# Attention heads by pairs: the half-array products of two heads given together, alternating between the halves of the TensorE array

## The chip, the cores and the metric

The kernel runs on one core of a Trainium2 chip, in one launch. The metric is the device time of that core in microseconds (us), the median of the runs of a kernel.

## What is computed

Two layers' worth of a hybrid language model on 256 tokens of width 1024, in float32 (a sketch of the reference, cut to the parts that matter here):

```python
# first block
u_ssm, q, k, v = split(rmsnorm(x) @ w_in)
y_ssm  = s5_branch(u_ssm)          # recurrence over 256 tokens, 32 groups of 64 complex states, gelu, glu
y_attn = stick_breaking(q, k, v)   # 8 heads of 64:
#   z = q k^T / 8;  A = sigmoid(z) * prod_{s<j<t} (1 - sigmoid(z_j));  out = A v, s < t only
merged = g_ssm * (y_ssm @ w_up_ssm) + g_attn * (y_attn @ w_up_attn)    # g: sigmoid gates of u
h = x + merged @ w_out
h = h + relu(rmsnorm(h) @ w_ff1) ** 2 @ w_ff2
# second block, twice: gated feed-forward, a mixer, gated feed-forward
# the mixer: softmax attention (8 heads, 96 query and key features, 64 value features) beside a second
# attention with compressed and plain keys; gates; projections; layer norms
```

## The kernel before, in words

**Products.** Weights come from memory as float32 blocks. ScalarE copies half a block to its rounded high part (`high`, L538), VectorE subtracts to get the low part (`low`, L553), and a large product is three TensorE products of high and low parts (`mm3`, L590 to L592); "a trio" below. The small products of the attentions are plain float32, and the trace shows each of these as two passes.

**Heads on half the array.** A head of 64 features fills half of the 128 x 128 array. In `stick` (stick-breaking attention), the scores of head h (`sz`, L1268 and L1269) contract over 64 rows, the upper or the lower half by the head's parity; its output (`so`, L1308 and L1310) has 64 columns, left or right. In `mla_head` (the mixers' softmax attention) the output (`mo`, L1887 and L1888) has 64 columns as well. The rest of a head lies between them: in `stick` three ScalarE functions and three VectorE operations (tiles `sa`, `szs`), a cumulative sum as a product (`sc`, L1288 to L1290), two VectorE operations, an exponential.

**The order.** The engines run what stands in their queues in order. For the first block and each mixer, a planner (`Flow`) writes these orders when the program is built: streams (generators) state the engine, an estimated time and the buffers that the next piece needs; the piece that could start first by the planner's estimate is given out, the lower priority number winning among those that are close. Where TensorE would wait, it gives out trios of "fillers", in a fixed list: in the first block the input products, the eight gate products (`g0` to `g7`), then the glu (`lu`, L590 on tile `sg`), the attention's projection (`a0`, `a1`, on `oa`) and the recurrence's (`s0`, `s1`). The glu needs the gelu of the recurrence's outputs (`s5_gelu`: after all heads and all four groups), the attention's projection needs `joined` (all pairs and the gelu), the last two need the glu.

**Buffers.** Streams must hold tiles of the planner's lists: `t2` (4 at the start of the first block, 2 more come free in `s5_powers`, which keeps one), `acc` (5 PSUM tiles), `sunit` (1: one head of the stick-breaking attention at a time), `grp` (2 groups of the recurrence at a time). A head holds two `t2`, `sa` until `sc`, `szs` until `so`. A group of the recurrence (`s5_states`) takes one `t2` with its inputs' product (`s5b`, L1161), turns them on VectorE (L1152) and GpSimd (L1169, L1170), then needs two more `t2` at once for a factor (`s5r`, L1175) and the scans (L1179); it turns the result (L1152, GpSimd L1189 and L1190) and adds its outputs to PSUM (`ys`, L1205 and L1208). Heads have priorities 3 to 10, groups 8 to 11.

Of the kernel before, what the change touches and what calls it, by code (L numbers as in the profile page):

```python
# [17 lines left out]
P = 128  # L18
# [7 lines left out]
# The tail of a layer: its last TAIL row blocks, row by row; the products after which the first row's two  # L26
# halves are transposed, in feed-forward layers and in the others.
# [3 lines left out]
# Of Flow: buffers, priorities, and what it weighs (times in us).  # L31
# [10 lines left out]
# The first block's later products: gates, glu and the two projections.  # L42
LATE = "g0 g1 g2 g3 g4 g5 g6 g7 lu a0 a1 s0 s1".split()
# The weight stream: blocks loaded in halves, tiles split ahead, split blocks at a mixer's end.
# [3 lines left out]
# When a feed-forward layer's first hidden columns are turned (without and with gate), and when the  # L48
# weights of a mixer's first products are taken.
# [4 lines left out]
def host_constants():  # L54
    """Tables that depend on the shapes alone."""
# [39 lines left out]
class Halves:  # L95
    """Columns of a row in two tiles."""
# [10 lines left out]
class Row:  # L107
    """The end of a layer for 128 tokens: their sums on top of the residual, the norm
    (of the root mean square, or of mean and variance when there is a bias) and the
    feature-major split of the result."""  # L110
# [31 lines left out]
    def finish(self):  # L142
        """Up to the scale of the rows; then self.piece(c0, c1) writes the result."""
        k, nc, s, b = self.k, self.k.nc, self.s, self.b
        TS, STT = nc.vector.tensor_scalar, nc.vector.scalar_tensor_tensor
        m = self.n - 1
        if self.bB is None:
            TS(s(10), s(4), s(4 + m), self.eps, OP.add, OP.add)
            k.rsqrt(s(11), s(10))
            return  # L150
        TS(s(12), s(0), s(m), 1.0 / D, OP.add, OP.mult)
        TS(s(13), s(9), s(12), None, OP.add)
        TS(s(13), s(13), s(13), -self.eps, OP.mult, OP.add)
        TS(s(10), s(4), s(4 + m), s(13), OP.add, OP.subtract)  # L154
        k.rsqrt(s(11), s(10))
        for c in (slice(0, 512), slice(512, D)):
            STT(self.h[:, b, c], self.h[:, b, c], s(12), self.gB[:, c], OP.subtract, OP.mult)
# [12 lines left out]
    def turn(self, c0, c1, pool=None):  # L170
        """Transposes columns c0:c1 and splits the high parts; returns the low parts' step."""
# [12 lines left out]
    def early(self):  # L184
        """All of it but the transposes."""
# [8 lines left out]
    def late(self, head):  # L194
        """All of it, the next layer's work on the other tokens filling the wait."""
# [15 lines left out]
class FFHead:  # L211
    """The first 256 hidden columns of a feed-forward layer, token by token."""
# [40 lines left out]
class MixHead:  # L253
    """The first columns of a mixer's input product, token by token."""
# [21 lines left out]
def act(n, exp=False):  # L276
    """A ScalarE instruction's time, in us, for n columns."""
# [3 lines left out]
def dve(n, fast=False):  # L281
    """A VectorE instruction's time, in us, for n columns."""
# [3 lines left out]
class Flow:  # L286
    """An order of emission for streams of work that share the engines. A stream is a generator that
    yields (engine, time, resources...) before it emits that work, or the name of a signal to wait for;
    the next piece is the one that could start first by a model of the engines, and fillers (feature-major
    products) go where TensorE would wait. Each resource is a count of buffers with the times at which  # L290
    they come free."""
# [24 lines left out]
    def rest(self):  # L316
        """Puts off the current stream, whose products are too small to keep TensorE's clock up."""
# [6 lines left out]
    def start(self, s):  # L324
        """When a stream's next piece could start, or None."""
# [26 lines left out]
    def weight(self, e):  # L352
        """The next part of the weights' split, as a stream's piece."""
# [26 lines left out]
    def filler(self, t):  # L380
        """A step of the first filler."""
# [13 lines left out]
    def evac(self, engine, d, f):  # L395
        """Work that follows the filler's products."""
        self.evacs.append((self.free["PE"] + 0.65, engine, d, f))

    def open(self):
        """Whether a filler can go on."""  # L400
# [51 lines left out]
class Kern:  # L452
    def __init__(self, ctx, tc, A, out):
# [8 lines left out]
        self.blocks = []      # planned weight blocks, in the order of their use  # L462
        self.staged = []      # loaded, not yet split
        self.loaded = 0
        self.pieces = 0       # halves of blocks split so far
# [36 lines left out]
    def rowblk(self, w, r0, nk, c0, n):  # L502
        """nk chunks of 128 rows from r0, n columns from c0, as [128, nk, n]."""
# [26 lines left out]
    def high(self):  # L530
        """The high part of half a weight block."""
# [9 lines left out]
    def piece(self):  # L541
        """The low part of half a weight block, and the high part of the next."""
# [43 lines left out]
    def mm3(self, out, l, r, start, stop, **kw):  # L586
        """out (+)= l.T @ r, the operands split in high and low parts."""
# [6 lines left out]
    def split_from(self, hi, lo, src, scale=None):  # L594
        """hi, lo (float32r) from src (* scale)."""
# [8 lines left out]
    def fm_gen(self, key, xs, evac, alloc=None):  # L604
        """A feature-major block: [128, 256] sums per 128 columns, in PSUM tiles of
        two; evac(i, tile) follows each tile. Yields the tiles of work done."""
# [27 lines left out]
    def fill(self, tiles):  # L634
        """Emits about that much of the waiting work."""
# [9 lines left out]
    def tok_mm(self, o, w, xs, k0, b, c0, c1, first, last, **kw):  # L645
        """Adds a row block to the token-major sums o of the 128 tokens b, columns c0:c1."""
# [9 lines left out]
    def tok_first(self, o, ws, b, n):  # L656
        """The token-major sums o of n columns, the tokens' low parts last."""
# [15 lines left out]
    def tok_tail(self, accs, parts, rows, head, at):  # L673
        """The last row blocks (w, xs, k0): the first 128 tokens, then the others,
        each followed by the end of its row."""
# [24 lines left out]
    def bcast_row(self, src, n, name):  # L700
        """A row of DRAM on every partition."""
# [13 lines left out]
    def transpose_split(self, src, nchunk, xs):  # L715
        """src: [128 tok, 2, nchunk*128] -> split feature-major xs."""
# [155 lines left out]
    # The states' recurrence runs over 64 steps of four tokens each: state' = a^4 state + V [u], and  # L872
    # the outputs of a step are W state + K [u], with V, W and K made of B, C and the powers of a.
    # Its inputs and outputs sit on the partitions as (token of the step, channel of 32).
# [26 lines left out]
    def s5_powers(self, f):  # L901
        """The powers of a and what goes with them: s5c (parameters by state), pw, dk, tau4, r4."""
# [70 lines left out]
        def cmul(out, x, y, n):  # L973
            """out = x * y, complex; x: n numbers per state chunk, y: one."""
# [13 lines left out]
    def s5_part(self, f, dst, x, y, k, s0, s1):  # L988
        """dst (block-diagonal) = y_k * x; s0, s1: the signs' operations."""
# [13 lines left out]
    def s5_b(self, f):  # L1003
        """The states' inputs: bb (for K) and its transpose."""
# [20 lines left out]
    def s5_c(self, f):  # L1025
        """The outputs' weights by state, and their transpose for K."""
# [36 lines left out]
    def s5_turns(self, f):  # L1063
        """The steps' rotations."""
# [21 lines left out]
    def s5_k(self, f):  # L1086
        """K: row blocks by the token that enters, column blocks by the one that leaves."""
# [45 lines left out]
    def s5_in(self, ps, u4, q0):  # L1133
        """The products' columns (two blocks of 128 channels) as the steps' inputs."""
# [8 lines left out]
    def s5_states(self, f, g, u4, ys):  # L1143
        """Four chunks of 128 states (groups 8g to 8g + 7) over all steps, and their part of the outputs
        in the PSUM accumulators ys, two [128, 8, 64]."""
# [3 lines left out]
        def turn(m, v):  # L1149
            """m: the real and the imaginary parts v by cos and by sin."""  # L1150
# [62 lines left out]
    def s5_gelu(self, f, ys, out):  # L1213
        """gelu of the outputs, by channel and token, and its split."""
# [5 lines left out]
        # the steps' inputs, rotations and K are done with  # L1220
# [32 lines left out]
    def stick(self, f, h, qk, vt, O):  # L1253
        """One head of the stick-breaking attention; a pair's result takes its queries' place in qk."""
        nc = self.nc
        pair, hh = divmod(h, 2)
        rows = slice(64 * hh, 64 * hh + 64)
        q, k = qk[rows, pair, :], qk[rows, 4 + pair, :]
# [7 lines left out]
        yield "PE", 0.65, "acc", "t2", "t2", "sunit"  # L1266
        z = self.acc("sz")
        nc.tensor.matmul(z[:, :T], k[:, :P], q, start=True, stop=True)  # L1268
        nc.tensor.matmul(z[:, T:T + P], k[:, P:], q[:, P:], start=True, stop=True)  # L1269
        f.sig("sz%d" % h)  # L1270
# [4 lines left out]
        yield "ACT", 3 * act(384) + 0.4  # L1275
# [21 lines left out]
        nc.scalar.activation(zs, zs, AF.Exp)  # L1297
        f.sig("st%d" % h)
        yield "vt"
        if hh:  # L1300
            yield "so%d" % pair
            yield "PE", 0.65
        else:
            yield "PE", 0.65, "acc"
            O[pair] = self.acc("so")
        o = O[pair]
        hv = slice(h * 64, (h + 1) * 64)
        nc.tensor.matmul(o[rows, :T], vt[:, 0, hv], zs[:, :T], start=True, stop=False,  # L1308
                         tile_position=(0, 64 * hh))
        nc.tensor.matmul(o[rows, P:T], vt[:, 1, hv], zs[:, T:], start=False, stop=True,  # L1310
# [941 lines left out]
```

## Time and profile before

| | |
|---|---|
| median of 3 runs | 1560.99 us (1559.63 to 1564.06) |
| profiled execution, first to last instruction | 1560.2 us; the profile gives no other time of that execution |
| TensorE busy, products | 1534.7 us, 98% of the span |
| VectorE / ScalarE / GpSimd busy | 992.3 / 773.2 / 97.8 us (64 / 50 / 6%) |
| DMA | 265.24 MB, mean 170 GB/s |
| mean granted TensorE clock | 0.994 |

The stick-breaking heads and the recurrence run between about 48 and 168 us of the span, the glu and the projections from 177 to 205 us, the two mixers' heads around 660 to 695 and 1235 to 1263 us.

### The profile page before, as it was taken

How to read it: one execution, taken by the hardware profiler on the slowest of the kernel's cores; microseconds unless marked ns; L12 is line 12 of the kernel's file. 1: busy time of each engine (PE TensorE's matmuls, PEld its weight loads, DVE VectorE, ACT ScalarE, POOL GpSimd, SP SyncE). 2: the span in 40 equal slices, each digit the busy share in tenths (PEclk: the TensorE clock that was granted, in tenths of full speed). 3: DMA queues.
4: the chain of work that ended last, by engine and by line, in shares of the span. 5: the costliest groups of instructions: out<-in, count | busy, mean ns of one | idle time of the engine just before them, and what ended most of it. 6: DMA issues, size and time to landing. Idle time of an engine off the chain costs nothing.

```text
span 1560.2 us, 25562 instructions
## 1 busy us (share of the span) xinstructions
PE 1534.7 (98%) x10637; PEld 1418.5 (91%) x10637; DVE 992.3 (64%) x1572; ACT 773.2 (50%) x1259; POOL 97.8 (6%) x112
## 2 busy tenths in 40 slices
PE   8799999999999999999999999999999999999998
PEld 7699989989999998989999999999999999899997
DVE  7956776454654547778875445844557779864544
ACT  7455845444543435557654343534434567554342
POOL 2841000000000000000000000000000000000000
PEclk9899999999999999999999999999999999999999
DMA  7413355556564555532565655565546433565550
GB/s 215 154 62 122 136 197 186 197 172 207 179 225 163 186 183 176 192 103 88 188 216 189 204 175 189 191 210 170 185 152 216 136 108 125 181 225 189 188 190 28
DMA packets 188597, 265.24 MB, mean 170 GB/s; under 512 B 10441, under 2 KB 154817, under 8 KB 188482
## 3 DMA queue, kind: packets, MB, share of 16 engines
q1 hardware_dynamic: 186466, 256.27, 49.7%
q0 software_dynamic: 2016, 7.34, 1.4%
q8 instruction: 84, 1.38, 0.4%
q14 instruction: 31, 0.25, 0.0%
HBM read 262.55 MB, written 1.05 MB: 169 GB/s over the span
## 4 chain that ended last, share of the span: by engine, by line
PE 92%; DVE 4%; POOL 2%; ACT 1%; issue 1%; DMA 0%; DVEq 0%; SPq 0%; ACTq 0%
PE mm L590 16%; PE mm L591 16%; PE mm L592 16%; PE acc L591 8%; PE acc L592 8%; PE acc L590 8%; PE head L664 6%; DVE wsplit L553 1%; PE tp L177 1%; PE cps L1665 1%; PE in L590 1%; PE in L592 1%; PE in L591 1%; PE apt L1949 1%; PE mo L1887 1%
## 5 line engine op out<-in xcount | busy, mean ns | idle before, releaser
L553 DVE TENSOR_TENSOR wsplit<-st,wsplit 128x1024 fp32r<-128x1024 f32 (+1 forms) x482 | 562.0, 1210 | 184.4 <-ACT wsplit L538 184.0
L590 PE MATMUL mm<-xh,wsplit 128*128 128x256 f32 x2000 | 572.2, 286 | 0.0
L591 PE MATMUL mm<-xl,wsplit 128*128 128x256 f32 x2000 | 564.8, 282 | 0.0
L592 PE MATMUL mm<-xh,wsplit 128*128 128x256 f32 x2000 | 564.8, 282 | 0.0
L538 ACT ACTIVATE wsplit<-st 128x1024 fp32r<-128x1024 f32 (+1 forms) x482 | 471.7, 1036 | 30.6 <-DMA st<-in_ffn_wg_dram 11.9
L590 PEld LDWEIGHTS mm<-xh,wsplit 128*128 128x128 f32 x2000 | 378.9, 189 | 4.5 <-issue 1.1
L591 PEld LDWEIGHTS mm<-xl,wsplit 128*128 128x128 f32 x2000 | 379.0, 189 | 2.1
L592 PEld LDWEIGHTS mm<-xh,wsplit 128*128 128x128 f32 x2000 | 378.6, 189 | 0.2 <-DVE wsplit L553 0.2
L590 PE MATMUL acc<-wsplit,ffh 128*128 128x512 f32 x480 | 189.5, 395 | 0.0
L592 PE MATMUL acc<-wsplit,ffl 128*128 128x512 f32 x480 | 189.4, 395 | 0.0
L591 PE MATMUL acc<-wsplit,ffh 128*128 128x512 f32 x480 | 189.3, 394 | 0.0
L828 ACT ACTIVATE fff<-mm 128x512 f32<-128x512 f32 x55 | 32.9, 598 | 280.1 <-PE mm L592 280.1
L832 DVE TENSOR_TENSOR fff<-fff,mm 128x512 f32<-128x512 f32 x55 | 37.9, 688 | 174.4 <-PE mm L592 111.2
L598 ACT ACTIVATE ffh<-fff 128x512 fp32r<-128x512 f32 x55 | 34.8, 632 | 165.8 <-DVE fff L832 165.8
L592 PEld LDWEIGHTS acc<-wsplit,ffl 128*128 128x128 f32 x480 | 90.4, 188 | 21.0
L590 PEld LDWEIGHTS acc<-wsplit,ffh 128*128 128x128 f32 x480 | 90.4, 188 | 18.8
L591 PEld LDWEIGHTS acc<-wsplit,ffh 128*128 128x128 f32 x480 | 90.4, 188 | 18.7
L707 POOL TENSOR_TENSOR rowst<-rowst,neghalf 128x1 f32<-128x1 f32 x18 | 14.7, 817 | 1227.2 <-DVE rowst L154 946.8
L664 PE MATMUL head<-wsplit,xh 128*128 128x256 f32 (+2 forms) x416 | 66.1, 311 | 0.0
L664 PEld LDWEIGHTS head<-wsplit,xh 128*128 128x128 f32 x416 | 59.6, 188 | 3.5
L599 DVE TENSOR_TENSOR ffl<-fff,ffh 128x512 fp32r<-128x512 f32 x55 | 38.1, 693 | 38.4 <-ACT ffh L598 38.4
L181 ACT ACTIVATE xh<-tp 128x256 fp32r<-128x256 f32 (+1 forms) x46 | 18.6, 470 | 48.6 <-PE tp L177 48.6
(405 smaller groups left out, 1894.6 us busy)
## 6 DMA issues: line engine op xcount, KB each, us to landing
st<-in_ffn_wg_dram SPq DMA_DIRECT2D x44, 1024.0 KB, 5.6
st<-in_ffn_wu_dram SPq DMA_DIRECT2D x44, 1024.0 KB, 5.4
st<-in_ffn_wd_dram SPq DMA_DIRECT2D x44, 1024.0 KB, 5.0
st<-in_w_ff_dram SPq DMA_DIRECT2D x32, 1024.0 KB, 6.4
st<-in_w_in_dram SPq DMA_DIRECT2D x23, 1024.0 KB, 6.3
st<-in_w_out_dram SPq DMA_DIRECT2D x12, 1024.0 KB, 4.9
st<-in_w_gate_dram SPq DMA_DIRECT2D x8, 1024.0 KB, 5.5
st<-in_w_in_dram SPq DMA_DIRECT2D x10, 512.0 KB, 5.4
```

The lines of the kernel that those rows point to most:

```text
L177: nc.tensor.transpose(ps[:, c * P:(c + 1) * P], self.out[:, b, c0 + c * P:c0 + (c + 1) * P], k.ident)
L181: nc.scalar.activation(hi, v, AF.Copy)
L538: self.nc.scalar.activation(self.split[i][0][:, a, b], self.staged[i][:, a, b], AF.Copy)
L553: self.nc.vector.tensor_tensor(lo[:, a, b], st[:, a, b], hi[:, a, b].bitcast(F32), OP.subtract)
L590: nc.tensor.matmul(out, lh, rh, start=start, stop=False, **kw)
L591: nc.tensor.matmul(out, lh, rl, start=False, stop=False, **kw)
L592: nc.tensor.matmul(out, ll, rh, start=False, stop=stop, **kw)
L598: nc.scalar.activation(hi, src, AF.Copy)
L599: nc.vector.tensor_tensor(lo, src, hi.bitcast(F32), OP.subtract)
L664: self.nc.tensor.matmul(o, l, r, start=i == 0, stop=i == len(ops) - 1)
L828: nc.scalar.activation(f, ps, AF.Silu if gated else AF.Relu)
L832: nc.vector.tensor_tensor(f, f, ps, OP.mult)
```

## The change

In `stick`, the even head of a pair now asks for the scores' tiles of both heads (two `acc`) and gives out the four `sz` products, alternating between the halves of the array; the odd head takes its two `t2` when its first ScalarE function comes. The even head ends after its exponential; the odd head waits for both and gives out the four `so` products, alternating, after which both heads' `szs` and the one `sunit` are given back. So `sunit` now stands for a pair. In `mla_head` likewise: the odd head gives out the four `mo` products. The number and the shapes of products stay.

```diff
     def stick(self, f, h, qk, vt, O):
...
-        yield "PE", 0.65, "acc", "t2", "t2", "sunit"
-        z = self.acc("sz")
-        nc.tensor.matmul(z[:, :T], k[:, :P], q, start=True, stop=True)
-        nc.tensor.matmul(z[:, T:T + P], k[:, P:], q[:, P:], start=True, stop=True)
-        f.sig("sz%d" % h)
+        if hh == 0:
+            yield "PE", 0.9, "acc", "acc", "t2", "t2", "sunit"
+            for i in range(2):
+                O[h + i] = self.acc("sz")
+            for c in range(2):
+                for i, r in enumerate(half):
+                    q, k = qk[r, pair, :], qk[r, 4 + pair, :]
+                    nc.tensor.matmul(O[h + i][:, c * T:T + c * P], k[:, c * P:c * P + P], q[:, c * P:],
+                                     start=True, stop=True)
+            f.sig("sz%d" % h)
+        else:
+            yield "sz%d" % (h - 1)
+        z = O[h]
...
-        yield "ACT", 3 * act(384) + 0.4
+        yield ("ACT", 3 * act(384) + 0.4) + (("t2", "t2") if hh else ())
...
+        O[h] = zs
         f.sig("st%d" % h)
+        if hh == 0:
+            return
         yield "vt"
-        if hh:
-            yield "so%d" % pair
-            yield "PE", 0.65
-        else:
-            yield "PE", 0.65, "acc"
-            O[pair] = self.acc("so")
...
+        yield "st%d" % (h - 1)
+        yield "PE", 0.9, "acc"
+        o = self.acc("so")
+        for c in range(2):
+            for i, r in enumerate(half):
+                hv = slice((h - 1 + i) * 64, (h + i) * 64)
+                nc.tensor.matmul(o[r, c * P:T], vt[:, c, hv], O[h - 1 + i][:, c * T:T + c * P],
+                                 start=c == 0, stop=c == 1, tile_position=(0, 64 * i))
+        f.put("t2", "t2", "sunit")
...
     def mla_head(self, f, h, qkT, vm, out, om):
...
+        out[h] = pt
         if hh == 0:
-            yield "PE", 0.65, "acc"
-            out[pair] = self.acc("mo")
+            f.put("unit")
+            f.sig("pt%d" % h)
         else:
-            yield "mo%d" % pair
-            yield "PE", 0.65
-        o, r0 = out[pair], 64 * hh
...
+            yield "pt%d" % (h - 1)
+            yield "PE", 0.9, "acc"
+            o = self.acc("mo")
+            for c in range(2):
+                for i in range(2):
+                    r0 = 64 * i
+                    nc.tensor.matmul(o[r0:r0 + 64, c * P:T], vm[:, c, h - 1 + i],
+                                     out[h - 1 + i][:, c * T:T + c * P], start=c == 0, stop=c == 1,
+                                     tile_position=(0, r0), skip_group_check=True)
+            f.put("t2", "t2", "unit")
```

The planner moves much of the first block with it. Three places matter below. The first is the end of the heads. VectorE before, from the last head's last operation to the gelu's split (`s5y` are the copies of the gelu, L1243):

```order
L1294 SCALAR_TENSOR_TENSOR szs<-const_82,szs 128x2x128
L553 TENSOR_TENSOR wsplit<-st,wsplit 128x1024
L1243 COPY s5y<-s5g 32x256 x8
L1250 TENSOR_TENSOR sg<-s5y,sg 128x512
L553 TENSOR_TENSOR wsplit<-st,wsplit 128x1024
```

And with the change, directly after the last head's last operation:

```order
L1179 SCALAR_TENSOR_TENSOR s5s<-s5r,s5z 128x256 x2
L1152 TENSOR_TENSOR s5m<-s5s,csT 128x512 x2
L1179 SCALAR_TENSOR_TENSOR s5s<-s5r,s5z 128x256 x2
L1152 TENSOR_TENSOR s5m<-s5s,csT 128x512 x2
L553 TENSOR_TENSOR wsplit<-st,wsplit 128x1024 x2
L1152 TENSOR_TENSOR s5m<-s5b,csT 128x512 x4
L553 TENSOR_TENSOR wsplit<-st,wsplit 128x1024
L1179 SCALAR_TENSOR_TENSOR s5s<-s5r,s5z 128x256 x2
L1152 TENSOR_TENSOR s5m<-s5s,csT 128x512 x2
L1179 SCALAR_TENSOR_TENSOR s5s<-s5r,s5z 128x256 x2
L1152 TENSOR_TENSOR s5m<-s5s,csT 128x512 x2
L1243 COPY s5y<-s5g 32x256 x8
```

All four groups of the recurrence, which VectorE had done among the heads before, now have their scans behind the last head, and two of them their inputs too. On TensorE the same groups stand behind the last `so`: 14 trios, half of the first group's `ys`, 2 trios, and then, in a row:

```order
L1205 MATMUL ys<-u_184,s5kT 128x64
L1208 MATMUL ys<-s5x,s5wT 128x63 x2
L1205 MATMUL ys<-u_184,s5kT 128x64
L1208 MATMUL ys<-s5x,s5wT 128x63 x2
L1161 MATMUL s5b<-u_184,s5bT 128x64 x8
L1205 MATMUL ys<-u_184,s5kT 128x64
L1208 MATMUL ys<-s5x,s5wT 128x63 x2
L1205 MATMUL ys<-u_184,s5kT 128x64
L1208 MATMUL ys<-s5x,s5wT 128x63 x2
L1161 MATMUL s5b<-u_184,s5bT 128x64 x8
L590 MATMUL mm<-xh,wsplit 128x256
```

After that last row's 4 trios come the `ys` of the two late groups and at once the glu; the 4 trios are the last of the gate products. Before, all `ys` stood among the heads, and 26 trios stood between the last `so` and the glu.

The second place is ScalarE from the gelu's split to the tanh of the glu (`gl`) and the high part of the attention's result (`oah`). Before:

```order
L1248 ACTIVATE sg<-s5y 128x512
L538 ACTIVATE wsplit<-st 128x1024 x2
L1531 ACTIVATE oah<-H 128x1024
L1431 ACTIVATE gates<-mm,s5c 128x256 x2
L1465 ACTIVATE gates<-gates 128x4096
L538 ACTIVATE wsplit<-st 128x1024 x2
L1471 ACTIVATE gl<-gl 128x1024
```

With the change:

```order
L1248 ACTIVATE sg<-s5y 128x512 x2
L538 ACTIVATE wsplit<-st 128x1024
L1470 ACTIVATE gates<-gates 128x4096
L1476 ACTIVATE gl<-gl 128x1024
L1536 ACTIVATE oah<-H 128x1024
```

The attention's result is now split after the tanh of the glu instead of before it. VectorE follows: its part `oal` stood before the copies `gl`, and now stands behind them, two weight splits and one operation of the glu (`s5y`):

```order
L1451 TENSOR_SCALAR gl<-mm,s5c 128x256 x4
L553 TENSOR_TENSOR wsplit<-st,wsplit 128x1024 x2
L1478 SCALAR_TENSOR_TENSOR s5y<-gl,s5y 128x1024
L1538 TENSOR_TENSOR oal<-H,oah 128x1024
```

The third place is VectorE at the end of the recurrence's projection (`mt`: the merge of one tile of it), just before the output product `w_out`. Before:

```order
L602 SCALAR_TENSOR_TENSOR xl<-mt_1972,xh 128x512
L553 TENSOR_TENSOR wsplit<-st,wsplit 128x1024 x2
L1497 SCALAR_TENSOR_TENSOR mt_2018<-gates,mm 128x512
L1499 TENSOR_TENSOR mt_2018<-mt_2018,gates 128x512
L602 SCALAR_TENSOR_TENSOR xl<-mt_2018,xh 128x512
L1497 SCALAR_TENSOR_TENSOR mt_2023<-gates,mm 128x512
L1499 TENSOR_TENSOR mt_2023<-mt_2023,gates 128x512
L602 SCALAR_TENSOR_TENSOR xl<-mt_2023,xh 128x512
L553 TENSOR_TENSOR wsplit<-st,wsplit 128x1024 x7
```

With the change:

```order
L602 SCALAR_TENSOR_TENSOR xl<-mt_2012,xh 128x512
L1502 SCALAR_TENSOR_TENSOR mt_2017<-gates,mm 128x512
L1504 TENSOR_TENSOR mt_2017<-mt_2017,gates 128x512
L602 SCALAR_TENSOR_TENSOR xl<-mt_2017,xh 128x512
L553 TENSOR_TENSOR wsplit<-st,wsplit 128x1024 x10
```

By the last merge VectorE has made 45 weight halves before and 42 with the change; the 43rd and 44th are the first block of `w_out`.

## Rows read from the trace of the kernel before

**Rows 1.** The page: busy time of the engines, and the chain that ended last.

```profile
PE 1534.7 (98%) x10637; PEld 1418.5 (91%) x10637; DVE 992.3 (64%) x1572; ACT 773.2 (50%) x1259; POOL 97.8 (6%) x112
...
PE 92%; DVE 4%; POOL 2%; ACT 1%; issue 1%; DMA 0%; DVEq 0%; SPq 0%; ACTq 0%
```

**Rows 2.** TensorE's waits, whole span, the one at the glu: us, times, longest.

```profile
PE mm L591 <- DVE sg L1250: 0.7, 1, 0.7
```

**Rows 3.** Timeline of TensorE, 97 to 99.4: start, us, engine, line, operation.

```profile
97.20 0.28 PE L592 MATMUL mm<-xh,wsplit 128*128 128x256 f32 x1
97.41 0.65 PE L1308 MATMUL so<-szs,vt 128*64 128x256 f32 x2
...
98.21 0.70 PE L1268 MATMUL sz<-H 64*128 64x256 f32 x2
...
99.05 0.39 PE L590 MATMUL mm<-xh,wsplit 128*128 128x256 f32 x1
99.28 0.27 PE L591 MATMUL mm<-xl,wsplit 128*128 128x256 f32 x1
```

**Rows 4.** Timeline of TensorE, 1235.3 to 1237.2: two heads' outputs, one after the other in program.

```profile
1235.79 0.70 PE L1887 MATMUL mo<-apT,vm 128*64 128x256 f32 x3
...
1236.32 0.38 PE L1887 MATMUL mo<-apT,vm 128*64 128x256 f32 x1
...
1236.85 0.55 PE L1873 MATMUL apt<-const,ap 128*128 128x128 f32 x3
```

**Rows 5.** Timelines of VectorE and GpSimd, 117 to 124: one group of the recurrence.

```profile
117.50 1.26 DVE L1179 TENSOR_TENSOR_SCAN s5s<-s5r,s5z 128x256 f32<-128x256 f32 x2
118.69 1.26 DVE L1152 TENSOR_TENSOR s5m<-s5s,csT 128x512 f32<-128x512 f32 x2
...
120.12 0.74 POOL L1189 TENSOR_TENSOR s5x<-s5m 128x256 f32<-128x256 f32 x1 [5.98 <-DVE s5m L1152]
...
121.50 0.73 POOL L1169 TENSOR_TENSOR s5z<-s5m 128x256 f32<-128x256 f32 x1
...
122.87 0.62 POOL L1175 TENSOR_TENSOR s5r<-constt,s5q 128x256 f32<-128x256 f32 x1
```

**Rows 6.** Timeline of TensorE, 106 to 108.4: half of a group's `ys`, then the next product.

```profile
106.19 0.33 PE L1205 MATMUL ys<-u,s5kT 128*128 128x64 f32 x2
...
107.57 0.65 PE L1308 MATMUL so<-szs,vt 128*64 128x256 f32 x2
```

**Rows 7.** Timeline of ScalarE, 165 to 178: gelu, copies, split; then the attention's result.

```profile
166.43 1.09 ACT L1228 ACTIVATE s5g<-ys 128x512 f32<-128x512 f32 x2
...
167.66 5.43 ACT L1241 ACTIVATE s5y<-s5g 32x256 f32<-32x256 f32 x8
173.12 0.63 ACT L1248 ACTIVATE sg<-s5y 128x512 fp32r<-128x512 f32 x1
...
177.74 1.05 ACT L1531 ACTIVATE oah<-H 128x1024 fp32r<-128x1024 f32 x1
```

**Rows 8.** Timeline of VectorE, 166 to 184: two weight splits, the glu's copies.

```profile
177.21 2.36 DVE L553 TENSOR_TENSOR wsplit<-st,wsplit 128x1024 fp32r<-128x1024 f32 x2
...
182.55 0.88 DVE L1446 TENSOR_SCALAR gl<-mm,s5c 128x256 f32<-128x256 f32 x2 [1.07 <-PE mm L592]
```

**Rows 9.** Timeline of VectorE, 196 to 207: the merge of one tile.

```profile
196.80 0.69 DVE L1497 SCALAR_TENSOR_TENSOR mt<-gates,mm 128x512 f32<-128x512 f32 x1 [0.97 <-PE mm L592]
...
198.92 0.69 DVE L602 SCALAR_TENSOR_TENSOR xl<-mt,xh 128x512 fp32r<-128x512 f32 x1 [0.70 <-ACT xh L601]
```

**Rows 10.** Busy time by stretch: length; engines PE, PEld, DVE, ACT, POOL; granted clock.

```profile
48.90:51.25 2.35, 0.00 (x0) 0.00 (x1) 2.35 (x4) 2.33 (x4) 2.29 (x3) 0.97 0.37 89
51.25:57.90 6.65, 6.65 (x28) 6.24 (x28) 6.65 (x8) 4.68 (x6) 6.52 (x6) 0.50 0.36 126
...
73.10:78.40 5.30, 5.26 (x19) 4.57 (x20) 5.30 (x5) 2.49 (x3) 5.18 (x4) 0.50 0.61 185
```

**Rows 11.** The same view of TensorE alone, the fillers behind the last `so`.

```profile
166.30:175.70 9.40, 9.40 (x80) 1.00 0.31 113
```

More of the change, by code (lines that the diff above doesn't have):

```diff
@@ L1256, in stick @@
         pair, hh = divmod(h, 2)
-        rows = slice(64 * hh, 64 * hh + 64)
-        q, k = qk[rows, pair, :], qk[rows, 4 + pair, :]
+        half = (slice(0, 64), slice(64, P))
         def diag(a):
@@ L1297, in stick @@
         nc.scalar.activation(zs, zs, AF.Exp)
+        O[h] = zs
         f.sig("st%d" % h)
+        if hh == 0:
+            return
         yield "vt"
-        if hh:
-            yield "so%d" % pair
-            yield "PE", 0.65
-        else:
-            yield "PE", 0.65, "acc"
-            O[pair] = self.acc("so")
[L1306 to L1310, printed above, removed]
-                         tile_position=(0, 64 * hh))
-        f.put("t2", "sunit")
-        f.sig("so%d" % pair)
-        if hh:
-            yield "sz%d" % (h - 1)
-            yield "ACT", act(256)
-            nc.scalar.activation(qk[:, pair], o[:, :T], AF.Copy)
-            f.put("acc")
-            f.sig("sp%d" % pair)
+        yield "st%d" % (h - 1)
[7 more added lines that the diff above has]
+        f.put("t2", "t2", "sunit")
+        yield "ACT", act(256)
+        nc.scalar.activation(qk[:, pair], o[:, :T], AF.Copy)
+        f.put("acc")
+        f.sig("sp%d" % pair)
     def first_block(self):
@@ L1878, in mla_head @@
         f.put("acc")
+        out[h] = pt
         if hh == 0:
-            yield "PE", 0.65, "acc"
-            out[pair] = self.acc("mo")
-        else:
-            yield "mo%d" % pair
-            yield "PE", 0.65
-        o, r0 = out[pair], 64 * hh
-        kw = dict(tile_position=(0, r0), skip_group_check=True)
-        nc.tensor.matmul(o[r0:r0 + 64, :T], vm[:, 0, h], pt[:, :T], start=True, stop=False, **kw)
-        nc.tensor.matmul(o[r0:r0 + 64, P:T], vm[:, 1, h], pt[:, T:], start=False, stop=True, **kw)
-        f.sig("mo%d" % pair)
-        f.put("t2", "unit")
-        if hh == 1:
+            f.put("unit")
+            f.sig("pt%d" % h)
+        else:
+            yield "pt%d" % (h - 1)
[8 more added lines that the diff above has]
+            f.put("t2", "t2", "unit")
             if not om:
```

## Prediction

> **What bounds the kernel now.** The page first: TensorE is busy for 98% of the span and makes 92% of the chain that ended last [rows 1]. So whatever shortens TensorE's own work comes off the end, and whatever makes it wait is added. The list of its waits comes next: between the last head and the output product it waits for 0.7 us, at the glu [rows 2], since 26 trios cover the gelu. 80 products take 9.40 us there [rows 11], 0.12 each, 0.36 a trio. The timelines then give what a head's products cost alone and side by side [rows 3, 4], and what the work costs that the change moves out from under that cover [rows 5 to 9]. The busy time by stretch shows what a wait does to the clock [rows 10].
>
> **What the change takes off TensorE.** Alone, a head's `so` fills the time from 97.41 to 98.21, 0.80 us, and its `sz` that from 98.21 to 99.05, 0.84 us [rows 3]. Once, the old order already had two heads' outputs next to each other: in 1235.79 to 1236.85, 1.06 us, both are done, and the second head's first passes start before the first head's are through (three passes of L1887 in the first row) [rows 4]. The halves do work at the same time.
> - `so` and `mo`: 4 and 8 pairs, of which one is side by side already. 11 pairs by 2 x 0.80 - 1.06 = 0.54 us: 5.9 us. Rows 4 have one head behind the other and not alternating; I take the same for both orders.
> - `sz`: no row shows two row halves together. Between nothing and a whole head (0 to 4 x 0.84 = 3.4 us), I take the offset of rows 4, 0.26 us: 0.84 - 0.26 = 0.58 by 4 pairs, 2.3 us. Nearest row, same engine, same passes.
> - Borders: where a half-array product follows or precedes a full one, the next start is late: 0.21 us instead of 0.12 before, 0.23 instead of 0.12 behind [rows 3], 0.20 us together. Five such runs fewer in the first block, 1.0 us; in the mixers 7 fewer, half of them next to small products that have a border of their own: 0.7 us.
>
> In all 9.9 us less; bounds 1.7 (borders alone) and 12.
>
> The Trainium skill ("TensorE: Matmul & The Clock Gate", Part 3) gives packed tiles a span of one product's duration and some 4 ns for each further tile. By that a pair would cost 0.80 and not 1.06, and the forecast would be about 4 us lower; rows 4 measure 1.06, and I go by them.
>
> **What it adds: waits behind the last head.** A pair holds four `t2`, two heads' worth, and heads go before groups; a group that wants two more for its scans gets them when no pair is left. That is what the order shows: all scans, and the inputs of two groups, behind the last head. The first two groups' scans run under the 14 trios (5.0 us): scans and turns 1.26 each [rows 5], their `ys` come after the trios. From there TensorE meets four chains:
> 1. *The late groups.* Behind their inputs: 0.2 to hand over, turn 1.26, a weight split 1.18 (half of 2.36 [rows 8]), then scan and turn by starts 1.2 each (117.50 to 118.69), 0.15, GpSimd's pair 1.38 (120.12 to 121.50) [rows 5]: 6.6 us. GpSimd's own inputs (1.37 and 0.62) lie beside the split. TensorE has 4 trios, 1.4 us, and a first product, 0.2. Wait **5.0**.
> 2. *The gelu.* Behind the last `ys`: 0.2, half of 1.09, the copies 5.43, the split 0.63 [rows 7] and VectorE's part, 0.69 (a 128x512 operation, [rows 9]): 7.5. No filler is left. **7.4**, beside a first product.
> 3. *The attention's result.* Behind the glu: 0.2, `gl` 0.88, two splits 2.36 [rows 8], `s5y` and `oal` at the shape of a split, 1.18 each: 5.8. ScalarE's tanh and `oah`, about 1.05 each [rows 7], are through earlier. Less one product: **5.7**. Before, `oal` was made while the glu ran.
> 4. *The first weights of `w_out`.* Behind the last projection: 0.2, one merge 2.81 (196.80 to 199.61) [rows 9], one split 1.18: 4.2, less one product; 0.4 more for the second half: **4.4**. Before, VectorE was three halves ahead.
>
> Sum 22.5, less the old 0.7: **21.8 us**. None hides beside another, as each ends with TensorE starting the work that the next one waits for. Bounds: 15, if a split slips out of chains 1 and 3 and 4 is half covered; 25, if ScalarE is late too.
>
> **The clock.** Behind the 2.35 us without a product that end at 51.25, the granted clock stands at 0.50 for 6.65 us, the lower level of 1.2 GHz, although TensorE is busy all that time; after a second wait it is at 0.50 again, for 5.30 us and more [rows 10]. Work at 0.50 takes twice as long, so such a stretch costs up to 3.3 us. A longer wait covers part of it: of the 6.65 us, 6.65 - (wait - 2.35) are left behind it, 4.0, 1.6, 3.3 and 4.6 us, half of which is lost: **6.8 us**. Bounds 0 (0.7 us at the glu changed nothing) and 4 x 3.3 = 13.
>
> **What costs nothing.** In the middle, `sc` of each head still has ten trios or so (3.6 us) between it and `sz`, against three ScalarE and two VectorE steps; the second head's have more. Holding a first head's finished tile for its partner delays nobody but the groups, which are counted. In the mixers fillers go on to the end; if that cover had a hole, a step of a head of some 0.5 us would show, once or twice. Weight loads: the same blocks in the same order on SP's queue; they wait for VectorE's splits, not the other way.
>
> **The sum.** -9.9 + 21.8 + 6.8 = +18.7 us on the profiled 1560.2: 1578.9. The median of the runs, 1560.99, lies 0.8 above that span: **1580 us**. With every bound at its low end 1560.99 - 12 + 15 = 1564, at the high end 1560.99 - 1.7 + 25 + 13 = 1597.
>
> **Rivals.**
> - *The halves don't work together in alternation*: if each pass must wait for the one before when the half changes, only the borders merge, and the waits stay: 8.2 us more, 1588. For: no row shows the alternation, nor row halves. Against: rows 4. 10%.
> - *The cover holds* (faster): the four chains cost nothing because VectorE and GpSimd have been let go earlier than I reckon. Place: the scans of the first groups. It decides if they begin more than 6.6 us before the last `so` ends, so that the late groups' inputs come in before the trios are used up. Then the gelu is still behind the last `ys`, so this alone saves 5.0 + 2.0; it wins only if the clock also stays up and the trios slide behind the gelu: 1560.99 - 9.9 = 1551. Against: the order of a queue is fixed, and no filler stands behind the `ys`. 7%.
> - *Half of it*: chains 3 and 4 overlap with TensorE running at half speed behind chain 2, and the clock costs little: 1560.99 - 9.9 + 5.0 + 7.4 + 2 = 1566, the edge of no change. 10%, of which half within 0.3%.
> - *The forecast*, 73%: by its bounds 1568 to 1594.
>
> **The numbers.** A measurement of this kernel can tell about 0.3%, 4.7 us, from no change: slower means above 1565.7. Forecast, first rival and half of the third: 0.88. Within 0.3%: 0.05 of the third and 0.01 of the faster one, 0.06. Faster: 0.06. The range takes the forecast's bounds, the first rival and most of the third: 1566 to 1594.
>
> **What the profile would show.** Right: four waits of TensorE between about 160 and 215 us that weren't there, on `ys` behind GpSimd's `s5x`, on the glu behind VectorE's `sg`, on L591 with `oal`, on L591 of `w_out` with a weight split, some 22 us together; stretches at 0.50 behind them; `mo` and `so` pairs near 1.06 us; the mixers shorter by 4 to 5 us. Wrong: those waits missing or below 10 us, or pairs at 1.6 us. A time below 1560 would mean that the end of the first block is covered after all.

## The result, and the profile after

The changed kernel takes **1589.53 us** (median of 4 runs, 1588.67 to 1591.09) against 1561.42 us for the kernel before in the same session: a ratio of 1.0178, 95% interval 1.0164 to 1.0192. It is 28 us slower; the forecast was 1580, the range 1566 to 1594. The profiled execution took 1588.67 us, its span is 1586.9 us, 26.7 more than before.

Where the span went, by the start of the first transposition (`tp`, L177) behind each stage in the two timelines:

| stage | before | after | difference |
|---|---|---|---|
| first block, up to its end | 225.38 | 254.56 | +29.2 |
| feed-forward layers behind it, up to the first mixer | 225.38 to 631.00 | 254.56 to 664.40 | +4.2 |
| first mixer | 631.00 to 790.93 | 664.40 to 820.74 | -3.6 |
| second mixer | 1202.12 to 1360.74 | 1231.93 to 1387.49 | -3.1 |

What is not in the table took the same time in both, within 0.1 us.

The page of the changed kernel: busy time, the granted clock in 40 slices, the chain that ended last.

```profile
PE 1537.1 (97%) x10637; PEld 1424.4 (90%) x10637; DVE 996.0 (63%) x1572; ACT 776.6 (49%) x1259; POOL 100.9 (6%) x112
...
PEclk9999589999999999999999999999999999999999
...
PE 89%; DVE 5%; ACT 2%; POOL 2%; DMA 1%; issue 1%; SPq 0%; DVEq 0%; ACTq 0%; POOLq 0%
```

Against [rows 1], TensorE has no less busy time although pairs overlap, and less of the chain. The half-level work hides in "busy": the same products at half the clock.

TensorE's waits in 40:255 of the changed kernel (total, times, longest):

```profile
PE mm L590 <- ACT sg L1248: 6.7, 1, 6.7
PE sc L1297 <- DVE sa L1293: 6.6, 2, 6.1
PE ys L1208 <- POOL s5x L1189: 4.9, 1, 4.9
PE acc L591 <- DVE wsplit L553: 3.8, 1, 3.8
PE mm L590 <- ACT oah L1536: 3.1, 1, 3.1
...
PE mm L591 <- DVE oal L1538: 1.9, 1, 1.9
PE ys L1208 <- POOL s5x L1190: 1.1, 2, 0.7
PE s5ps L1017 <- POOL s5bb L998: 0.8, 1, 0.8
```

All four forecast waits are there. Before, all waits of this part, to its end at 226, sum to 9.9 us, now to 31.7: **+21.8 us**.

Two timelines of TensorE in the changed kernel, a pair of the first block and one of the second mixer:

```profile
96.30 0.87 PE L1318 MATMUL so<-szs,vt 128*64 128x256 f32 x8
97.10 0.92 PE L1274 MATMUL sz<-H 64*128 64x256 f32 x8
97.95 0.39 PE L590 MATMUL mm<-xh,wsplit 128*128 128x256 f32 x1
...
1265.93 0.87 PE L1896 MATMUL mo<-apT,vm 128*64 128x256 f32 x8
1266.73 0.52 PE L1670 MATMUL cps<-cblk,cw 128*128 128x30 f32 x3
```

From start to next start a pair's `so` takes 0.80 us, its `sz` 0.85, its `mo` 0.80. That is what one head took alone [rows 3]; the second head is free.

The granted clock in the changed kernel, in the stretches at the lower level and in the one ahead of the second (columns as in [rows 10]):

```profile
60.96:67.79 6.83, 5.73 (x19) 4.97 (x20) 6.76 (x8) 1.12 (x2) 6.62 (x7) 0.50 0.23 81
150.20:156.53 6.33, 5.61 (x51) 5.48 (x50) 4.11 (x4) 0.00 (x0) 3.46 (x3) 1.00 0.13 28
156.53:166.77 10.24, 10.24 (x50) 10.24 (x50) 3.07 (x5) 1.85 (x2) 2.39 (x4) 0.50 0.22 85
170.19:194.08 23.89, 14.53 (x64) 13.86 (x65) 8.68 (x16) 10.80 (x13) 4.18 (x5) 0.50 0.07 23
200.91:207.73 6.82, 4.86 (x21) 4.57 (x22) 2.49 (x3) 2.89 (x4) 0.00 (x0) 0.50 0.45 154
231.63:238.45 6.82, 6.02 (x14) 4.72 (x15) 6.42 (x6) 1.73 (x2) 0.00 (x0) 0.50 0.55 186
```

TensorE's busy time at 1.2 GHz is 5.73 + 10.24 + 14.53 + 4.86 + 6.02 = 41.4 us; if that work takes half at full level, 20.7 us are lost. The same view of before, its two stretches:

```profile
51.10:57.93 6.83, 6.68 (x28) 6.27 (x29) 6.83 (x9) 4.82 (x7) 6.70 (x6) 0.50 0.37 129
71.58:78.41 6.83, 5.59 (x20) 4.62 (x21) 6.83 (x6) 2.49 (x3) 6.70 (x5) 0.50 0.71 227
```

12.3 us, 6.1 lost. The difference is **14.6 us**, twice the forecast's 6.8. "Half" is a little too much: at 0.50 a trio takes 0.64 us (from 165.00 in this run) against 0.36 [rows 11], and sixteen `s5b` passes take 3.41 us (`gated` below, from 108.25) against 1.79 (`gated_seq`, from 106.89), so 1.8 to 1.9 times as long. By that the term is an estimated 13 to 14 us. Behind the last head alone the half level costs 17.8 us, counted as half; 3.3 came back ahead of it, where one stretch stands instead of two.

Why the groups were late, in GpSimd's timeline of the changed kernel:

```profile
141.69 1.52 POOL L1175 TENSOR_TENSOR s5r<-constt,s5q 128x256 f32<-128x256 f32 x1 [50.93 <-PE sc L1299]
```

GpSimd stood for 50.93 us before the first group's factor `s5r`, the operation that needs two more `t2`, and a head's `sc`, which gives one back, ended that. The first scan then waited on VectorE for the last heads' `so`, which gives back `szs`:

```profile
145.31 1.65 DVE L1179 TENSOR_TENSOR_SCAN s5s<-s5r,s5z 128x256 f32<-128x256 f32 x2 [1.64 <-PE so L1318]
```

So tiles were what the first group lacked. No run gave the planner more of them, so how much of the delay the heads' priority alone would cause is not shown. The scans of all four groups (the tile `s5s`), in the kernel before (duration min, median, max; first and last start):

```profile
L1179 DVE TENSOR_TENSOR_SCAN s5s<-s5r,s5z x8: 665/676/692, 87.7 to 130.1; 128x256 f32<-128x256 f32 x8
```

and in the changed kernel:

```profile
L1179 DVE TENSOR_TENSOR_SCAN s5s<-s5r,s5z x8: 676/1091/1211, 145.3 to 171.7; 128x256 f32<-128x256 f32 x8
```

The last heads' outputs ended at 145.1 us (166.3 before): the heads were done 21 us sooner, and the first scan began only there.

### The profile page after: what moved, and what is told of

It is laid out like the page before. It is cut to its first block, busy times and chain, and to the rows that moved or that the text cites. A ratio compares the mean times of both kernels' runs of the same rounds, so it can differ in the third digit from the quotient of the medians.

```text
span 1586.9 us, 25517 instructions
## 1 busy us (share of the span) xinstructions
PE 1537.1 (97%) x10637; PEld 1424.4 (90%) x10637; DVE 996.0 (63%) x1572; ACT 776.6 (49%) x1259; POOL 100.9 (6%) x112
## 4 chain that ended last, share of the span: by engine, by line
PE 89%; DVE 5%; ACT 2%; POOL 2%; DMA 1%; issue 1%; SPq 0%; DVEq 0%; ACTq 0%; POOLq 0%
PE mm L590 15%; PE mm L591 15%; PE mm L592 15%; PE acc L592 9%; PE acc L591 9%; PE acc L590 8%; PE head L664 5%; DVE wsplit L553 1%; PE cps L1670 1%; PE tp L177 1%; PE in L590 1%; PE in L591 1%; PE in L592 1%; PE apt L1957 1%; PE s5b L1161 1%
## 5 line engine op out<-in xcount | busy, mean ns | idle before, releaser
L592 PEld LDWEIGHTS acc<-wsplit,ffl 128*128 128x128 f32 x480 | 90.4, 188 | 21.5 <-DVE ffl L599 0.4
L591 PEld LDWEIGHTS acc<-wsplit,ffh 128*128 128x128 f32 x480 | 90.4, 188 | 18.7
```

The lines of the kernel that those rows point to most:

```text
L591: nc.tensor.matmul(out, lh, rl, start=False, stop=False, **kw)
L592: nc.tensor.matmul(out, ll, rh, start=False, stop=stop, **kw)
```

## The experiments

Theory: the pairs save what a second head cost. The loss comes from the order: pairs hold the `t2` tiles, the groups slide behind the last head, and the waits and the half-level stretches behind them cost more than is saved. Rivals: two heads at a time leave the engines no room in any order; alternation itself disturbs the clock. Diffs are against the changed kernel unless said otherwise.

### m_only and s_only: one half of the change alone

`m_only` has the whole old `stick` (first diff, its core), `s_only` the whole old `mla_head` (second):

```diff
     def stick(self, f, h, qk, vt, O):
...
-            yield "PE", 0.9, "acc", "acc", "t2", "t2", "sunit"
...
+        yield "PE", 0.65, "acc", "t2", "t2", "sunit"
+        z = self.acc("sz")
...
```

```diff
     def mla_head(self, f, h, qkT, vm, out, om):
...
-            yield "pt%d" % (h - 1)
-            yield "PE", 0.9, "acc"
...
+            yield "mo%d" % pair
+            yield "PE", 0.65
...
```

> Pairs in the mixers alone, the stick-breaking heads as before. Theory (a pair costs what one head costs, 0.80 us, and the mixers have no other effect): the two mixers lose 6.7 us together, so 1561.4 - 6.7 = 1554.7 us, and the first block stays as before. Rival (a pair costs 1.06 us, as the prediction had it): 4.4 us, 1557.0. If the mixers' gain in the changed kernel came from something the first block did, below 2 us: above 1559.

> Pairs in the stick-breaking attention alone, the mixers as before. Theory (all that is lost lies in the first block and the feed-forward layer behind it, the mixers gain on their own): 1589.5 + 6.7 = 1596.2 us. Rival (the parts are not additive, the mixers' pairs also cost something there): 1590 to 1593.

Measured: `m_only` 1555.64 us, ratio to before 0.9957 (0.9945 to 0.9969); its mixers are 3.7 and 3.1 us shorter. `s_only` 1597.37 us, ratio 1.0225 (1.0212 to 1.0239). Against 1562.0 us for before in that session the parts are -6.4 and +35.4 and add up to +29.0; the whole change measured +28.1. All of the loss comes from `stick`.

### gated: the same pairs, the groups given turns

The signal `gs` comes when a group's scans are given out (in `s5_states`); the next pair (in `stick`) waits for it in the planning:

```diff
         f.put("t2", "t2")
+        f.sig("gs%d" % g)
...
         if hh == 0:
+            if pair:
+                yield "gs%d" % (pair - 1)
             yield "PE", 0.9, "acc", "acc", "t2", "t2", "sunit"
```

> Both pairs kept; each pair of stick-breaking heads after the first waits, when the order is planned, until a group of the recurrence has had its scans (pair 1 for group 0, and so on), so that groups get their t2 tiles between pairs. No product, size or buffer changes. Theory (the loss is the groups' lack of t2, which puts them behind the last head): the waits at ys, at the glu and at the projections of some 17 us and the half-level stretches of some 14 us behind them go, the first block is near before less 7.6 us for the products and about 1 us more at the first sc; with the mixers' 6.7 us about 1548 us, 40 trios stand before the glu. Rival 1 (two heads at a time leave VectorE and ScalarE no room for the groups whatever the order): the waits move among the pairs, 1570 to 1585. Rival 2 (alternating halves lower the clock by themselves): the granted clock still falls to 0.5 between 145 and 195 us, above 1560.

Measured: 1552.0 us (median of 9), ratio 0.9953 (0.9933 to 0.9972): faster than before, with the products, sizes and buffers of the changed kernel. The scans of `gated`:

```profile
L1179 DVE TENSOR_TENSOR_SCAN s5s<-s5r,s5z x8: 665/692/1153, 99.0 to 148.5; 128x256 f32<-128x256 f32 x8
```

They lie among the heads again. None of the four waits is left in TensorE's list; its longest rows in `gated`:

```profile
PE sc L1300 <- DVE sa L1296: 4.6, 1, 4.6
PE tp L177 <- DVE xl L182: 2.4, 1, 2.4
PE sz L1277 <- ACT H L1399: 2.4, 1, 2.4
...
PE acc L590 <- ACT ffh L598: 1.5, 1, 1.5
```

The theory holds and the first rival falls. In the second rival's place, 145 to 195 us, the clock stays up: it is at 1.00 from 126.2 to 230. But the executions fall into two groups: five at 1550.9 to 1552.0 us (mean clock 0.995 to 0.997), four at 1558.9 to 1561.2 (0.988 to 0.990). The profiled one is of the second kind. Its busy time by stretch:

```profile
101.50:105.80 4.30, 3.51 (x28) 3.00 (x27) 4.30 (x6) 4.15 (x9) 3.39 (x4) 1.00 0.42 143
105.80:126.20 20.40, 20.40 (x96) 20.22 (x95) 7.50 (x13) 6.36 (x14) 4.51 (x6) 0.50 0.00 0
```

and the same stretches of `gated_seq` (below), where the order of the groups is the same:

```profile
101.50:105.80 4.30, 3.62 (x30) 3.19 (x29) 4.30 (x6) 4.15 (x9) 3.57 (x4) 1.00 0.39 132
105.80:126.20 20.40, 20.40 (x175) 19.71 (x175) 13.33 (x21) 12.45 (x26) 4.43 (x6) 1.00 0.21 62
```

The same 20.4 us, all of it busy, hold 96 products at half level or 175 at full. The fall came behind a stretch of 64-column `ys` products with 0.8 us of waits in it. By these counts it costs 9.2 us, which is also the distance between the medians of the two groups. Without the fall `gated` lies 3 us above its forecast of 1548; the feed-forward layers behind it, which take 4.4 us more than before, account for that. That the other three fell at the same place is told by their times and mean clocks alone.

### gated_warm: is it what runs there that lowers the clock?

To `gated`, a method that gives out products of 128x512 whose results nobody reads, called in `s5_states` behind every three `ys` products of the first group:

```diff
+    def warm(self, n):
+        ps = self.mm("warm")
+        for _ in range(n):
+            self.nc.tensor.matmul(ps, self.xs[0][:, 0, :P], self.xs[0][:, 0:2], start=True, stop=True)
...
+            if g == 0:
+                self.warm(2)
```

> The kernel 'gated' with eight added products of 128x512 (1.9 us) among the twelve ys products of its first group, at 102 to 107 us, where the clock fell in the profiled execution and, by the times, in 4 of 9. Theory (the small products and two short waits there lower the clock in some executions): it falls in none; all runs within 3 us of each other, median about 1553 us. Rival (the fall has nothing to do with what runs there): again about half of the runs near 1561 us.

Measured: 1553.94 us, all five executions between 1552.76 and 1554.93, mean clock 0.994 to 0.996, and 1.00 from 101.5 to 126.2 in the profile. With 1.9 us more work none is near 1560 us, although the two short waits there stayed (0.15 and 0.63 us). That agrees with the theory and does not prove it: at 4 falls in 9, five executions in a row without one come by chance once in 19, and `gated` was not run beside it.

### warm_small and warm_wait: small products or waits?

The same question for the changed kernel's own falls. `warm_small`, behind every three `ys` products and behind every second `s5b` product of groups 2 and 3. That is 24 added products, 16 of them before the late groups' `ys`, and not the 32 and 24 that its forecast counts:

```diff
+            self.warm(1)
...
+            if g > 1:
+                self.warm(1)
```

`warm_wait`, ahead of group 2's `ys`, and in `s5_gelu` behind the last `ys`:

```diff
+        if g == 2:
+            yield "PE", 0.1
+            self.warm(18)
...
+        yield "PE", 0.1
+        self.warm(26)
```

> The changed kernel with 32 products of 128x512 added whose results nobody reads: one behind every three ys products, one behind every s5b product of the two late groups. Theory (the run of 64-column products behind the last head lowers the clock at 156.5): the clock stays at 1.00 there; the added 24 products before 165 take 5.5 us and the stretch 5.1 less, the ys behind the late groups take 7.3 instead of 10.7 us; the glu behind the gelu's wait still runs at half: about 1586 us. Rival (only TensorE's waits lower the clock, the small products do nothing): the clock still falls near 156.5, and the added products cost 7 us at full and up to 12 us at half level: 1597 to 1602.

> The changed kernel with products of 128x512 added in two of its waits: 18 before the ys of the late groups, 26 before the glu; nobody reads them. Theory A (waits lower the clock): the fall at 156.5 stays, but from 170 to 194 the clock is at 1.00, the work there takes 7 us less: 1582 us. Theory B (the run of small products lowers it): it is at 0.5 again during the 24 small ys products, and the added products run at half level beyond the waits: 1588 to 1594 us.

Measured: `warm_small` 1591.8 us (1.0189, 1.0173 to 1.0204), `warm_wait` 1585.14 us (1.0148, 1.0134 to 1.0162), the changed kernel 1589.5. Busy time by stretch in `warm_small`:

```profile
150.00:165.00 15.00, 15.00 (x120) 14.41 (x119) 8.07 (x9) 2.08 (x4) 7.39 (x7) 1.00 0.22 72
...
172.50:195.00 22.50, 14.88 (x57) 13.22 (x58) 7.36 (x14) 7.64 (x12) 4.08 (x5) 0.50 0.07 24
```

and in `warm_wait`:

```profile
159.00:166.00 7.00, 7.00 (x34) 7.00 (x34) 1.72 (x3) 0.50 (x1) 1.97 (x3) 0.50 0.13 50
...
175.50:186.00 10.50, 10.50 (x43) 9.68 (x43) 2.88 (x8) 3.48 (x6) 1.83 (x3) 0.51 0.13 50
186.00:195.00 9.00, 9.00 (x61) 8.26 (x60) 2.42 (x5) 8.00 (x8) 0.00 (x0) 1.00 0.00 0
```

With large products among the small ones the clock is at 1.00 through 150 to 165, where it had fallen at 156.5; it falls behind the 5.6 us wait that follows. With large products in the waits the first fall comes near 158, the clock is up again over the filled wait, and it falls at 175.5 within the 24 small `ys` products, behind two short waits (0.23 and 0.63 us); the glu behind the filled second wait runs at 1.00.

So the clock can fall in a run of 64-column products that has no single wait above 0.72 us in it. But `warm_small` does not show that its large products kept it up, because `s_only` needs none. Its first block has the changed kernel's order, and its profiled execution ran the same products, behind the same 0.7 us wait, at the upper level:

```profile
158.04:165.00 6.96, 6.96 (x61) 6.96 (x62) 2.13 (x4) 0.91 (x1) 1.98 (x3) 1.00 0.44 151
```

There the clock fell at 168.1, in the 5.8 us wait for the late groups. In one and the same order the small products go before a fall in one execution and not in another; what decides it is open. `warm_small` lies between its two numbers: its eight last added products, like the `ys` and the glu, ran at half level behind the wait. `warm_wait` lies between A and B.

### warm_both: inconclusive

The edits of `warm_small` and `warm_wait` together, 68 added products.

> Both sets of added products. Theory (waits and small products each lower the clock, and the half level costs some 12 us between 156 and 195): no fall between 145 and 195 us although TensorE has 17 us more work, so about 1580 us. Rival (the clock falls for another reason and the half level is not what costs): the added products outlast the waits: above 1595 us.

Measured: 1585.1 us (1.0153, 1.0139 to 1.0167). The clock is at 1.00 until about 175, falls there all the same, behind 2.1 us of waits for `s5x`, and is back at 1.00 from about 189. It lies between both numbers. That the half level is some 14 us of the loss is thus a count from the busy times. The two groups of `gated` bear out the price of one stretch; no run alone prices the term in the changed kernel.

### gated_seq: head by head instead of alternating

Against `gated`, in each of the three places where a pair's products are given out:

```diff
-            for c in range(2):
-                for i, r in enumerate(half):
+            for i, r in enumerate(half):
+                for c in range(2):
```

> As gated, but the four products of a pair stand head by head (both of the first, then both of the second) and not alternating. Theory (it is alternation that makes a pair as short as one head; head by head it takes the 1.06 us of the row of before): 12 output pairs by 0.26 us and 4 score pairs by at most 0.26 us more than gated, 3 to 4 us slower, and 1.06 us a pair in the trace. Rival (standing together is enough): within 1 us of gated, 0.80 us a pair.

Measured: 1549.29 us, ratio 0.9924 (0.9912 to 0.9935). Not slower at all. A pair in its timeline:

```profile
120.09 0.88 PE L1321 MATMUL so<-szs,vt 128*64 128x256 f32 x8
120.89 0.93 PE L1277 MATMUL sz<-H 64*128 64x256 f32 x8
121.75 0.39 PE L590 MATMUL mm<-xh,wsplit 128*128 128x256 f32 x1
```

Again 0.80 and 0.86 us. The theory falls, the rival holds: standing together is enough, and alternating gives nothing beyond it. (Against the five executions of `gated` without a fall, 1551.2 us, it is 1.9 us faster and not within 1; the same kernel run again, below, took 1551.3.) (The first pair's `so` takes 0.92 us; its cause stays open.) Then why had [rows 4] 1.06 us? ScalarE's timeline of the kernel before at that place tells:

```profile
1235.13 0.87 ACT L1877 ACTIVATE apT<-apt 128x384 f32<-128x384 f32 x2 [0.58 <-PE apt L1873]
```

The two heads' `apT` were made one after the other, the second done at 1236.00. The second head's first pass, the last of the three in 1235.79 to 1236.49, lasts 0.43 us and so started at 1236.05. The 0.26 us was a late operand, not the price of a half.

### gated_seq_again: did the clock just happen to stay up?

The same kernel once more.

> The kernel 'gated_seq' once more. 'gated' had 4 of 9 executions near 1560 us, where the clock fell at 106 us, 'gated_seq' none of 5. Theory (the fall is a matter of a few tenths of a us at a point where both orders are alike, so 'gated_seq' was lucky): 1 to 3 of 5 near 1559 us. Rival (head by head the clock keeps up there): all within 1548 to 1553 us.

Measured: 1551.3 us (1549.46 to 1552.82), ratio 0.9938 (0.9924 to 0.9951). By times and mean clocks, no fall in 10 executions of `gated_seq`, against 4 of 9 in `gated`: the rival holds as stated. `gated` was not run again beside it, so whether the order by heads keeps the clock up there, and by what, stays open; with that, so does whether alternation has a part in that fall.

### gated_urgent: the feed-forward layer's 3 to 4 us

Against `gated_seq`:

```diff
-URGENT = 20
+URGENT = 30
```

> As 'gated_seq', but weight halves count as urgent when fewer than 30 tiles (before 20) are split ahead, so VectorE stands 2 halves further ahead at the first merges. Theory (the 3 to 4 us that all kernels with paired stick-breaking heads lose in the first feed-forward layer, where ScalarE waits for w_ff's loads, come from splits that were put off among the heads): that layer is 2 to 3 us shorter, about 1547 us. Rival (the loads come too late because the first block got shorter and the same bytes have to come in less time): the layer stays, 1549 us, or worse by a new order of the heads.

Measured: 1560.88 us (median of 12; seven at 1558.1 to 1561.5, five at 1567.5 to 1569.8), ratio 1.0012 (0.9994 to 1.003). As a whole a miss. For its question it is clear: from the first block's end (225.38 before) to the first transposition behind the layer (408.80), before takes 183.4 us, the changed kernel 186.3, `gated_seq` 186.0, `gated_urgent` 183.4. The other 1.3 us of the changed kernel's 4.2 lie in the layer after that, and are gone in `gated_urgent` too. What ScalarE waited for in that layer, in the changed kernel:

```profile
ACT wsplit L538 <- DMA st<-in_w_ff_dram: 64.2, 14, 4.9
ACT fff L828 <- PE mm L592: 13.1, 14, 1.9
```

and in `gated_urgent`:

```profile
ACT fff L828 <- PE mm L592: 74.7, 15, 5.5
ACT ffh L598 <- DVE fff L832: 11.3, 15, 0.8
```

These two numbers are those of before as well. With the splits given out sooner the waits for loads are gone, and the layer is as long as before. That points to late splits. Too little time for the bytes does not explain it: the changed kernel, whose first block is 29 us longer, has the waits too. But the new number moved other work as well: the first block gained 5 instead of 10 us, the first mixer nothing, and the second lost 2.3.

## Why the prediction was right, point by point

The sign, the mechanism and the place were right: all four chains appear, in the forecast order, and each wait is near its price. The forecast of 1580 lies 9.5 us below the measured time, 8.0 of it on the span. Three terms were off, one of them the other way. The products lie outside their own bounds and the clock at or above the top of its own; the range held because these two errors pull against each other and the range reached 14 us above the forecast. That is luck in part, and so is the equal sum of the waits.

| term | forecast | measured |
|---|---|---|
| products of pairs | -9.9 (bounds -1.7 to -12) | -13.9 (in the first block, what the other terms leave) |
| waits in the first block | +21.8 | +21.8 |
| clock | +6.8 (0 to 13) | +14.6 (counted as half; estimated 13 to 14) |
| feed-forward layers | 0 | +4.2 |
| sum on the span | +18.7 | +26.7 |

- **Products.** The mixers lost 6.7 us. In the first block 29.2 = 21.8 + 14.6 - 7.2; counted directly, 4 `so` by 0.80, 4 `sz` by 0.85 and 1.0 of borders are 7.6. With the lower estimate of the clock, 1 to 2 us of this balance have no place yet. The failed step is "in 1235.79 to 1236.85, 1.06 us, both are done" as the price of a pair: it was the arrival of an operand. The Trainium skill ("TensorE: Matmul & The Clock Gate", Part 3) lets packed tiles span one product's time plus a few ns. The trace agrees: 0.80 us for two heads. By that sentence the forecast would have been an estimated 4 us lower, further from the result, since the other terms were short.
- **Late groups**: 5.0 forecast, 4.9 for the main wait, with the smaller ones 6.0. **Gelu**: 7.4 against 6.7, ended by ScalarE's half of the split. **Attention's result**: 5.7 against 3.1 + 1.9; the first of the two ended with ScalarE's `oah`, which the forecast had called through earlier. **First weights of `w_out`**: 4.4 against 3.8. Together 21.5 for 22.5.
- **"In the middle ... costs nothing"** failed for the first pair: its `sc` waits took 4.2 us more, as the two heads' ScalarE and VectorE steps have only 10 trios of cover. 2.7 us fewer waits at `s5ps` beside it hid that in the sum. For the later pairs it held.
- **The clock** is the term that was mis-sized most. The forecast gave each wait one stretch of the length in [rows 10] behind it. In its place 10.24 busy us at half level came in a run of `ys` and `s5b` products behind only 0.7 us of waiting, where no chain stands, and 14.53 more, `ys` again and some 17 of the glu's 48 products, in one stretch of 23.89 us across two waits. `s_only` had the first of these at full level and the second longer (16.71 busy us in 27.31), so the single stretches vary between executions.
- **"Weight loads ... they wait for VectorE's splits, not the other way"** names the right order and was still priced wrong: as `gated_urgent` suggests, splits were put off in the first block, so the loads behind them came late, and the next layers paid 4.2 us.
- **The rivals.** Halves that don't work together: a pair would take 1.6 us; it takes 0.80. A cover that holds: the scans would have to begin 6.6 us before the last `so` ends; they begin behind it. Half of it: chains 3 and 4 cost 8.8 us and the clock 13 us or more.

## What to carry to other kernels

When two units of work are merged, ask which buffers the merged unit holds and who else needs two of them at once: here a saving of 14 us became a loss of 28 us through tiles that one `yield` claims, and a signal between pairs turned it into a gain of 10 to 13 us, where the clock did not fall, with no product added or left out. Before a spacing in a trace is taken for the price of a resource, look when the later operand was written. A stretch of small products can cost clock without any long wait, in some executions and not in others, so a forecast should give it a range; that large products among them prevent it is likely from `gated_warm` and not proven.

## What was not expected of the hardware

- Head by head in program order, both heads' 256-column products still run side by side, and the second head's overtake the first head's 128-column one. `gated_seq`, the tile `so` in 120:120.5:

```profile
L1321 PE MATMUL so<-szs,vt x4: 379/404/430, 120.1 to 120.4; 128*64 128x256 f32 x4
```

  Four passes of 256 columns, those of both heads, start before any of 128 columns, though the program's order is 256, 128, 256, 128. Across the two halves, then, products did not start in the order of TensorE's queue.
- The granted clock fell while TensorE was busy: in the profiled execution of `gated` it fell at 105.8 us, 1.7 us behind the last short wait, and stood at 0.50 for 20.4 us without a gap. By its times the same program fell in 4 of 9 executions. The changed kernel's fall at 156.5 us is missing in `s_only`, which has the same order there.
